# Fourth tile for transposed values, pauses in the modulation products, a longer lead for split weights and later norm products

## Chip, cores and metric

One Trainium2 chip, one of its cores. The metric is the device time of one execution in microseconds (us). Six engines matter: TensorE (PE in the profile, with its weight loads shown apart as PEld), VectorE (DVE), ScalarE (ACT), GpSimd (POOL) and SyncE (SP), whose queue issues every DMA of this kernel.

## What is computed

Two models in a row on 256 tokens of width 1024. The first block has two layers; each is a gated feed-forward (hidden width 2816), a hybrid mixer and a second feed-forward:

```
for l in range(DEPTH):                      # DEPTH = 2
    x = x + 0.5 * swiglu_ffn(rmsnorm(x, norm_ffn1[l]), ...)
    x = x + hybrid_mixer(rmsnorm(x, norm_mix[l]), ...)
    x = x + 0.5 * swiglu_ffn(rmsnorm(x, norm_ffn2[l]), ...)
```

The second block also has two layers. Both are modulated by products of a conditioning vector with a large matrix, `mod = silu(c) @ ada_w[i] + ada_b[i]`, once for the 256 tokens and once for 256 context tokens. Its first layer is a recurrence over time (`wkv_scan`, 16 heads of width 64, forward and backward), its second a differential attention. All of it is float32.

## The kernel before

**Layout and products.** Features lie on the partitions, tokens along the free dimension. A float32 product is made of three products in the float32r type: weights and operands are split into a high part and a low remainder (`whi`, `wlo` in the first block, `vhi`, `vlo` in the second), and high by high, high by low and low by high are added in PSUM (`mm3`, line 484). ACT makes the high part of a weight (`emit_hi`), DVE the low one (`emit_lo`, a subtraction of two SBUF tensors). A tile of the first block's weights is 128 by 1024, split in two pieces of 512 columns; it feeds 8 blocks of three products.

**The order of the instructions** is fixed when the program is built, by a planner. `Clock` holds an estimated time for each engine. `mm3` emits its three products and then calls `tick`, which lets every waiting chain whose estimated time has come emit its next step, and lets `Weights.tick` split more weights: a piece is emitted if its estimated time is below the PE clock plus `W.ahead` (2000 ns in the feed-forwards, 2000, 4000 and 2000 ns in the parts of a mixer), and if the ring has room (`RING`: 4 raw tiles, 5 split ones). A chain is a Python generator: work that hangs on one result, such as `swiglu` (line 697), the residual or a norm, and each `yield` ends a step. Tiles are taken with `grab` and returned with `give`; a chain that finds none waits. On the chip each engine runs its own list in order, so an instruction that waits holds up all that stand behind it.

**A feed-forward** (`ffn`, line 688) makes 44 products of 8 blocks each ("up": tiles a0, b0, a1, b1 ... b21), then 8 products of 22 blocks each ("down", n = 0 to 7). `done(j)` is called at the end of up-tile j and starts `swiglu(f)` after every second one; that chain needs the norm's factor `row.rstd`. Down product n = 0 needs all 22 results of `swiglu`, the last one in its last block. The passages spoken of below are the one from up to down and the one from a stage to the next, where the residual of n = 7 must be added before the next stage's norm and its last operand block are there.

**The norm.** `entered` (line 591) writes the split operand and adds squares on POOL into `sq`. After the eighth, `rstd_chain` (line 527) emits the PE product `ps<-mean,sq`, an addition on DVE, a power on POOL, a second PE product `ps<-ident,small` that spreads the factor over the partitions, and a copy into `rstd`; then `row.ready` is set.

**The modulation products** are chain `ada` (line 1094): 96 times a load of 256 KB, a POOL product of 128 by 1024 (`ada<-adaw,ada`) and two ACT sums. It is not urgent, starts 90 us in by the planner's clock, and takes a new product only while `self.calm` is true:

```
for n, (l, i, h) in enumerate(work):
    yield
    while not self.calm or there[n] > self.clock.t["PE"]:
        yield
```

`ffn` sets `calm` at its start and keeps it until down product 7; the mixers leave it false.

**The recurrence** (`rwkv`, line 1354) goes over eight pairs of heads j. Each has a chain `prepare`, two chains `products` (u = 0 for the context, u = 1 for the tokens), then `inverse` (small triangular inverses) and `recur` (eight steps, four for u = 0 and four for u = 1; each copies `rs` once). One set of tiles serves `inverse`, one `recur`. `products` ends with its own u's values: it transposes `q` four blocks at a time (`q<-ps` on ACT), grabs a tile `uv`, transposes `vp` (`ps<-ident,vp`) and copies the result into it:

```
uv, = yield from self.grab("uv")
```

`inverse` of a pair starts when both of its `products` have ended. `recur` gives a `uv` back after the four steps of its u. There are three such tiles (`NUV`).

Of the kernel before, what the change touches and what calls it, by code (L numbers as in the profile page):

```python
# [18 lines left out]
KD = 8  # L19
DFF = 2816  # L20
KF = DFF // 128
# [5 lines left out]
class Clock:  # L27
# [22 lines left out]
    def pressing(self):  # L50
# [6 lines left out]
        left = ((k + 1) * self.TICK - now) * (2.4 if fast else 1.2)  # L57
        short = self.FULL + PUSH - done
        if not 0 < short <= left:
# [79 lines left out]
class Part(tuple):  # L139


    t = 0.0
# [182 lines left out]
class Base:  # L325
# [66 lines left out]
    def between(self):  # L392

        if self.ranked and not (PUSH is not None and self.clock.pressing()):
            self.advance()

    def until(self, cond):
        n = 0
        t = self.clock.t
        while not cond():  # L400
            now = t["PE"]
            if self.tick():
                n = 0
            if t["PE"] == now:
                t["PE"] += 60
            n += 1
            assert n < 3000, (self.chains, {k: len(v) for k, v in self.free.items()})
# [76 lines left out]
    def mm3(self, ps, w, k, n0, xs, start, stop):  # L484
# [6 lines left out]
        if self.pace:  # L491
            self.paced = max(self.paced, self.clock.t["PE"] - SLACK) + self.pace
        wh, wl = hv[:, k, n0:n0 + 128], lv[:, k, n0:n0 + 128]
# [5 lines left out]
        mm(ps, wl, xs[0], start=False, stop=stop)  # L499
        self.tick(press=self.ranked and PUSH is not None and self.clock.pressing())  # L500

# [25 lines left out]
    def rstd_chain(self, row, ps=None):  # L527

        nc = self.nc
        m = row.n // 128  # L530
        summed = ps is not None
        if not summed:
            ps, = yield from self.grab("ps")
        s, = yield from self.grab("sm")
        if not summed:
            for t in range(m):
                nc.tensor.matmul(ps[:, 2 * t:2 * t + 2], row.sq[:, t * 128:(t + 1) * 128], self.mean,
                                 start=True, stop=True)
            yield
        nc.vector.tensor_scalar(out=s[:, 0:2 * m], in0=ps[:, :2 * m], scalar1=1e-6, scalar2=None, op0=ALU.add)  # L540
        yield
        nc.gpsimd.tensor_tensor(out=s[:, 8:8 + m], in0=s[:, 0:2 * m:2], in1=self.mhalf[:, :m], op=ALU.pow)
        yield
        for t in range(m):
            nc.tensor.matmul(ps[:, t * 128:(t + 1) * 128], s[:, 8 + t:9 + t].to_broadcast([128, 128]),
                             self.ident, start=True, stop=True)
        yield
        nc.vector.tensor_copy(row.rstd, ps[:, :row.n])
        self.give(s, kind="sm")
        self.give(ps, kind="ps")  # L550
        if row.half is not None:
            nc.scalar.activation(row.half, row.rstd, AF.Copy, scale=0.5)
        row.ready = True

    def square_sum(self, row, k, src):

        nc = self.nc
        if k == 0:
            row.ps, = yield from self.grab("ps")
            row.summed = 0  # L560
        s, = yield from self.grab()
        nc.scalar.activation(s[:, :row.n], src, AF.Square)
        yield
        while row.ps is None:
            yield
        row.summed += 1
        for t in range(row.n // 128):
            nc.tensor.matmul(row.ps[:, 2 * t:2 * t + 2], s[:, t * 128:(t + 1) * 128], self.mean,
                             start=row.summed == 1 and t == 0, stop=row.summed == KD, skip_group_check=True)
        self.give(s)  # L570
        if row.summed == KD:
            yield
            yield from self.rstd_chain(row, row.ps)
# [38 lines left out]


SLACK = 6000.0
PUSH = 0
MOST = 40
COST = 41, 47, 105, 77, 220, 200
# [7 lines left out]
class First(Base):  # L625
# [61 lines left out]

    def ffn(self, W, tag, l, after):
        nc = self.nc
        self.calm = True  # L690
        V, A = nc.vector, nc.scalar
        self.until(lambda: 0 in self.operand)
        xs = Lazy(self.operand, self.until, KD)
        hs = [[self.space(2 * i + j, F32R) for j in range(2)] for i in range(KF)]
        ready = {}

        def swiglu(pa, pb, f):
            while not self.row.ready:
                yield
            t, = yield from self.grab()  # L700
            h = t[:, :T]
            V.tensor_tensor(out=h, in0=pa[:, :T], in1=self.row.rstd, op=ALU.mult)
            self.give(pa, kind="ps")
            yield
            A.activation(h, h, AF.Silu)
            yield
            V.tensor_tensor(out=h, in0=h, in1=pb[:, :T], op=ALU.mult)
            self.give(pb, kind="ps")
            yield
            yield from self.hi_lo(*hs[f], h)  # L710
            ready[f] = self.part(*hs[f])
            self.give(t)

        held = {}

        def done(j, ps):
            held[j] = ps
            if j % 2:
                self.chain(swiglu(held.pop(j - 1), held.pop(j), j // 2))

        keys = [(tag, l, ab, i, 0) for i in range(KF) for ab in "ab"]
        self.product(W, keys, xs, done)
        if tag == "f2" and l == 1:
            self.enter_ctx()
        hl = Lazy(ready, self.until, KF)
        for n in range(KD):
            self.calm = n < KD - 1
            ps = self.take("ps")
            for k0 in (0, 8, 16):
                w = W.get((tag, l, "d", n, k0 // 8))  # L730
                for k in range(k0, min(k0 + 8, KF)):
                    self.mm3(ps[:, :T], w, k - k0, 0, hl[k], k == 0, k == KF - 1)
            self.chain(self.residual(n, ps, self.row.half, after))
# [53 lines left out]
    def mixer(self, W, l, after):  # L787
        nc, big = self.nc, self.big
# [175 lines left out]
        for t in range(NH):  # L964
            if t % 4 == 0:
                wg = W.get(("wax", l, t))
                n = min(4, NH - t)
# [17 lines left out]
            w = W.get(("gate", l, t, 0))  # L985
            self.gemm([(w, 0)], xs, lambda _, ps: self.chain(gate(t, ps)))
        W.lo_pool, W.hi_pool = MIXLO[3]
        W.ahead = 2000
        until(lambda: (3, 2) in pooled)
        for i in range(4):  # L990
            w = W.get(("pu", l, i))
            for j in range(2):
                n = 2 * i + j
# [38 lines left out]
HALF = [slice(64 * e, 64 * e + 64) for e in range(2)]  # L1032


NQ, NGE, NUV, NSH, NS, NPP = 8, 2, 3, 1, 9, 1
PACE, PACE_FROM = 0.0, 1
URGENT, RANKS = (1, 1, 1), (0, 0, 0, 0, 0)
NAQ = 12
# [1301 lines left out]
```

## Time and profile before

| what | us |
|---|---|
| median of 3 runs | 2267.69 |
| lowest and highest | 2259.29 and 2274.60 |
| profiled execution, its own time | 2270.05 |
| span of that execution in the trace | 2268.3 |

The span runs from the first to the last instruction. By the trace, the first block takes it up to about 1300 us (feed-forwards at 19 to 225, 435 to 658, 658 to 871 and 1080 to 1266 us, mixers between), the recurrence about 1300 to 2023 us, the attention the rest. A row of a stretch gives the busy time of each engine in it; "PEclk" is the share of its full clock that TensorE was granted, where 1.00 is 2.4 GHz and the lower of its two levels is 1.2 GHz. In a row of the timeline, the bracket at the end is the idle time of the engine before the instruction and what ended it.

### The profile page before, as it was taken

To read this page: it belongs to the slowest core of one execution; us is meant where nothing else is said; L and a number is where in the kernel's file an instruction comes from. 1 tells how busy PE (TensorE), PEld (TensorE's weight loads), DVE (VectorE), ACT (ScalarE), POOL (GpSimd) and SP (SyncE) were. 2 spreads that over 40 slices of the span, in tenths; PEclk is the share of its full clock that TensorE was granted. 3 is DMA by queue.
4 is the path that set the end of the run, shared out by engine and by line. 5 is a ranking of instruction groups with operands and counts; after the bars stand their busy time and mean duration, and the time that the engine had idled before them with its cause. 6 is when DMAs were issued, how large, how long until landed. Compare 5 with 4: busy or idle time off the path is not lost.

```text
span 2268.3 us, 46757 instructions
## 1 busy us (share of the span) xinstructions
PE 2076.7 (92%) x18172; PEld 1878.2 (83%) x18172; DVE 1704.9 (75%) x2903; ACT 1251.4 (55%) x2802; POOL 862.3 (38%) x1092
## 2 busy tenths in 40 slices
PE   7988998998889889989999988999899889889998
PEld 7988988998889789989999966777677667667787
DVE  6689898888888888898666666675775773657896
ACT  6666585666666666765556554343344342336665
POOL 1144555344454453562001144543552542312231
PEclk9999999999999999999999997897887887869999
DMA  7666454666666565545656310010110110215442
GB/s 244 205 188 201 157 167 127 211 217 196 199 212 210 190 199 191 157 151 188 199 187 179 121 61 29 25 43 30 34 33 29 32 40 29 62 41 159 138 130 85
DMA packets 114095, 300.38 MB, mean 132 GB/s; under 512 B 12624, under 2 KB 18512, under 8 KB 113744
## 3 DMA queue, kind: packets, MB, share of 16 engines
q1 hardware_dynamic: 113872, 297.39, 41.4%
q8 instruction: 142, 2.33, 0.4%
q14 instruction: 81, 0.66, 0.1%
HBM read 292.89 MB, written 4.46 MB: 131 GB/s over the span
## 4 chain that ended last, share of the span: by engine, by line
PE 53%; DVE 21%; ACT 9%; issue 8%; POOL 5%; DMA 3%; SPq 0%; ACTq 0%; DVEq 0%; POOLq 0%
PE ps L89 53%; DVE wlo L89 8%; ACT ada L89 3%; DVE t L89 3%; ACT whi L89 3%; DVE b L89 2%; DMA adaw<-in_ada_w_dram 2%; POOL ada L89 2%; DVE X L89 1%; DVE q L89 1%; DVE invN L89 1%; DVE ops L89 1%; DVE GE L89 1%; POOL invt L89 1%; POOL invX L89 1%
## 5 line engine op out<-in xcount | busy, mean ns | idle before, releaser
L89 PE MATMUL ps<-ops,whi 128*128 128x256 f32 x4852 | 893.1, 282 | 18.3 <-ACT ops L89 9.1
L89 DVE TENSOR_TENSOR wlo<-wraw,whi 128x512 fp32r<-128x512 f32 (+2 forms) x792 | 675.8, 891 | 147.5 <-ACT whi L89 142.5
L89 PEld LDWEIGHTS ps<-ops,whi 128*128 128x128 f32 x4852 | 756.6, 190 | 22.2 <-ACT ops L89 9.3
L89 PE MATMUL ps<-ops,wlo 128*128 128x256 f32 x2504 | 709.1, 283 | 29.1 <-DVE wlo L89 28.7
L89 ACT ACTIVATE whi<-wraw 128x512 fp32r<-128x512 f32 (+2 forms) x798 | 437.7, 597 | 127.3 <-issue 59.2
L89 PEld LDWEIGHTS ps<-ops,wlo 128*128 128x128 f32 x2504 | 475.5, 190 | 37.1 <-DVE wlo L89 36.8
L89 PE MATMUL ps<-b,whi 128*128 128x256 f32 x1580 | 322.3, 290 | 31.9 <-ACT b L89 17.1
L89 POOL TENSOR_TENSOR ada<-adaw,ada 128x1024 f32<-128x1024 f32 x96 | 237.7, 2476 | 266.0 <-ACT ada L89 184.7
L89 PEld LDWEIGHTS ps<-b,whi 128*128 128x128 f32 x1580 | 261.8, 197 | 36.5 <-ACT b L89 17.9
L89 PE MATMUL ps<-ops,vhi 128*128 128x512 f32 (+1 forms) x624 | 227.4, 441 | 0.0
L89 PE MATMUL ps<-b,wlo 128*128 128x256 f32 x712 | 206.1, 290 | 8.9 <-DVE wlo L89 5.4
L89 DVE TENSOR_TENSOR vlo<-vraw,vhi 128x512 fp32r<-128x512 f32 x202 | 144.8, 731 | 24.5 <-ACT vhi L89 21.3
L89 POOL TENSOR_TENSOR sq<-sq,t 128x256 f32<-128x256 f32 x49 | 45.2, 922 | 279.3 <-ACT t L89 278.8
L89 POOL TENSOR_TENSOR small<-small,mhalf 128x8 f32<-128x8 f32 (+3 forms) x62 | 72.3, 1169 | 204.6 <-DVE small L89 202.1
L89 PEld LDWEIGHTS ps<-b,wlo 128*128 128x128 f32 x712 | 139.7, 196 | 12.2 <-DVE wlo L89 8.2
L89 ACT ACTIVATE ada<-ada 128x512 f32<-128x512 f32 (+1 forms) x193 | 120.6, 626 | 51.9 <-POOL ada L89 51.3
L89 PEld LDWEIGHTS ps<-ops,vhi 128*128 128x128 f32 x624 | 120.6, 206 | 25.7 <-issue 0.7
L89 ACT ACTIVATE vhi<-vraw 128x512 fp32r<-128x512 f32 x202 | 121.5, 619 | 28.9 <-PE ps L89 16.6
L89 PE MATMUL ps<-ops,vlo 128*128 128x512 f32 (+1 forms) x312 | 135.0, 433 | 0.2 <-DVE vlo L89 0.2
L89 PE MATMUL ps<-vhi,ops 128*128 128x512 f32 x384 | 127.7, 413 | 1.8 <-DVE ops L89 1.1
L89 POOL TENSOR_TENSOR Sd<-S,small 64x128 f32<-64x128 f32 x61 | 27.5, 451 | 196.5 <-DVE S L89 194.5
L89 ACT ACTIVATE b<-t 128x256 fp32r<-128x256 f32 (+1 forms) x104 | 42.4, 413 | 101.8 <-DVE t L89 101.7
(314 smaller groups left out, 3433.1 us busy)
## 6 DMA issues: line engine op xcount, KB each, us to landing
wraw<-in_ffn_w_up_dram SPq DMA_DIRECT2D x175, 512.0 KB, 3.9
wraw<-in_w_in_dram SPq DMA_DIRECT2D x80, 512.0 KB, 3.7
wraw<-in_ffn_w_down_dram SPq DMA_DIRECT2D x64, 512.0 KB, 3.6
adaw<-in_ada_w_dram SPq DMA_DIRECT2D x96, 256.0 KB, 4.0
vraw<-in_da_in_dram SPq DMA_DIRECT2D x96, 256.0 KB, 2.7
vraw<-in_rw_in_dram SPq DMA_DIRECT2D x60, 256.0 KB, 2.6
wraw<-in_ffn_w_down_dram SPq DMA_DIRECT2D x32, 384.0 KB, 3.8
wraw<-in_w_lru_up_dram SPq DMA_DIRECT2D x32, 320.0 KB, 2.9
```

The lines of the kernel that those rows point to most:

```text
L89: return call(*args, **kw)
```

## The change

It has four parts, and a setting that makes room for one.

- `NUV` is 4: a fourth `uv` tile (2 KB per partition) in the recurrence. `dynamic_dma_scratch_size=1024` is passed when the program is set up; it shrinks an area in SBUF.
- `calm` is no longer set at the start of `ffn` but in `swiglu`, once the norm's factor is there; it is cleared after up-tile 38 (a19), five up-tiles ahead of the down products, and stays false in down product 0 as it did in 7.
- `W.ahead` becomes 5000 from up-tile 8 of each feed-forward, and in the last part of a mixer, in place of 2000.
- A norm whose squares were added on POOL puts off its first PE product by 2000 ns of the planner's PE clock, and its second by 1000 ns. `rstd_chain` is used so in the first block, for the context's norm and for the tokens' norm ahead of the attention.

```diff
         if not summed:
+            yield from self.later(LATER[0])
             for t in range(m):
...
         nc.gpsimd.tensor_tensor(out=s[:, 8:8 + m], in0=s[:, 0:2 * m:2], in1=self.mhalf[:, :m], op=ALU.pow)
         yield
+        if not summed:
+            yield from self.later(LATER[1])
         for t in range(m):
...
+    def later(self, ns):
+
+        t = self.clock.t["PE"] + ns
+        while self.clock.t["PE"] < t:
+            yield
...
+LULL, LEAD = 3, 5000
+LATER = 2000, 1000
...
     def ffn(self, W, tag, l, after):
         nc = self.nc
-        self.calm = True
...
             while not self.row.ready:
                 yield
+            if f < KF - LULL:
+                self.calm = True
             t, = yield from self.grab()
...
             held[j] = ps
+            if j == 8:
+                W.ahead = LEAD
+            if j == 2 * (KF - LULL):
+                self.calm = False
...
         for n in range(KD):
-            self.calm = n < KD - 1
+            self.calm = 0 < n < KD - 1
...
         W.lo_pool, W.hi_pool = MIXLO[3]
-        W.ahead = 2000
+        W.ahead = LEAD
...
-NQ, NGE, NUV, NSH, NS, NPP = 8, 2, 3, 1, 9, 1
+NQ, NGE, NUV, NSH, NS, NPP = 8, 2, 4, 1, 9, 1
...
-    nc = _bacc.Bacc("TRN2", target_bir_lowering=False, num_devices=1)
+    nc = _bacc.Bacc("TRN2", target_bir_lowering=False, num_devices=1, dynamic_dma_scratch_size=1024)
```

## Rows read from the trace of the kernel before

**Rows 1.** Stretches, the feed-forwards: busy PE, PEld, DVE, ACT, POOL; PEclk; DMA.

```profile
19.30:225.00 205.70, 192.98 (x1594) 190.40 (x1594) 162.20 (x280) 126.36 (x284) 64.01 (x106) 0.98 0.65 202
...
435.00:658.00 223.00, 198.35 (x1615) 194.03 (x1615) 192.36 (x235) 145.12 (x359) 106.34 (x49) 0.98 0.63 202
658.00:871.00 213.00, 192.50 (x1559) 188.98 (x1560) 181.22 (x231) 139.48 (x344) 94.98 (x44) 0.96 0.64 206
...
1080.00:1266.00 186.00, 186.00 (x1582) 185.85 (x1581) 123.01 (x237) 105.45 (x212) 13.04 (x15) 1.00 0.57 180
```

**Rows 2.** The same stretches, the modulation products' tiles alone (ACT, POOL).

```profile
19.30:225.00 205.70, 27.16 (x77) 47.34 (x19) 0.98 0.65 202
435.00:658.00 223.00, 53.13 (x160) 99.10 (x40) 0.98 0.63 202
658.00:871.00 213.00, 49.17 (x148) 88.35 (x36) 0.96 0.64 206
```

**Rows 3.** Waits of PE, 0 to 1301 us: total, times, longest.

```profile
PE ps L89 <- DVE wlo L89: 34.1, 40, 2.6
PE ps L89 <- ACT b L89: 17.1, 4, 6.2
PE ps L89 <- POOL sq L89: 12.1, 3, 6.7
```

**Rows 4.** Timeline of PE: up to down in the second feed-forward, then a norm.

```profile
587.53 0.58 PE L89 MATMUL ps<-b,whi 128*128 128x256 f32 x1 [6.22 <-ACT b L89]
589.99 0.58 PE L89 MATMUL ps<-b,whi 128*128 128x256 f32 x1 [1.88 <-DVE b L89]
...
659.88 1.02 PE L89 MATMUL ps<-mean,sq 128*128 128x2 f32 x4 [6.74 <-POOL sq L89]
```

**Rows 5.** Stretch of down products after that passage.

```profile
590.00:650.00 60.00, 60.00 (x480) 60.00 (x481) 54.81 (x67) 40.11 (x100) 31.18 (x16) 0.95 0.67 210
```

**Rows 6.** Timeline of DVE and POOL around one modulation product.

```profile
469.60 0.69 DVE L89 TENSOR_TENSOR wlo<-wraw,whi 128x512 fp32r<-128x512 f32 x1 [1.01 <-ACT whi L89]
...
471.35 2.53 DVE L89 TENSOR_TENSOR wlo<-wraw,whi 128x512 fp32r<-128x512 f32 x1 [0.72 <-ACT whi L89]
...
470.93 2.41 POOL L89 TENSOR_TENSOR ada<-adaw,ada 128x1024 f32<-128x1024 f32 x1 [3.81 <-ACT ada L89]
```

**Rows 7.** DVE groups, 495 to 570 us, then 1100 to 1175 us: busy, mean ns, idle.

```profile
L89 DVE TENSOR_TENSOR wlo<-wraw,whi 128x512 fp32r<-128x512 f32 x44 | 48.7, 1139 | 8.8 <-ACT whi L89 8.5
...
L89 DVE TENSOR_TENSOR wlo<-wraw,whi 128x512 fp32r<-128x512 f32 x54 | 34.9, 688 | 18.7 <-ACT whi L89 18.7
```

**Rows 8.** Timeline of ACT and DVE, pair 1; last, the copy of `q` of pair 2.

```profile
1411.60 0.58 ACT L89 ACTIVATE q<-ps 128x512 f32<-128x512 f32 x1
...
1430.38 0.91 ACT L89 ACTIVATE uv<-ps 64x512 f32<-64x512 f32 x2 [0.61 <-PE ps L89]
...
1431.53 1.93 DVE L89 STREAM_TRANSPOSE invN<-GE 32x1024 f32<-32x1024 f32 x1
...
1490.05 0.64 ACT L89 ACTIVATE q<-ps 128x512 f32<-128x512 f32 x1
```

**Rows 9.** Timeline of ACT, `recur`: first steps of pairs 0, 1, 7; a long step.

```profile
1405.61 0.36 ACT L89 ACTIVATE rs<-ps 64x256 f32<-64x256 f32 x1
...
1477.54 0.38 ACT L89 ACTIVATE rs<-ps 64x256 f32<-64x256 f32 x1 [1.12 <-PE ps L89]
...
1978.29 0.38 ACT L89 ACTIVATE rs<-ps 64x256 f32<-64x256 f32 x1 [2.89 <-PE ps L89]
...
1591.44 0.38 ACT L89 ACTIVATE rs<-ps 64x256 f32<-64x256 f32 x1 [1.88 <-PE ps L89]
1602.57 0.38 ACT L89 ACTIVATE rs<-ps 64x256 f32<-64x256 f32 x1 [5.77 <-PE ps L89]
```

**Rows 10.** Stretches of the recurrence: seven periods, and one piece without `recur`.

```profile
1405.00:1978.00 573.00, 527.57 (x6035) 413.73 (x6034) 361.81 (x672) 222.81 (x492) 245.68 (x445) 0.84 0.11 36
...
1864.00:1897.00 33.00, 27.25 (x461) 22.54 (x456) 16.95 (x27) 8.07 (x17) 12.86 (x20) 0.53 0.01 1
```

## Prediction

> **What bounds the kernel now.** I read it by stages, since the page's shares average over two quite different halves.
>
> The stretches of the four feed-forwards come first [rows 1]. They make the same products: some 1584 large ones each. The last takes 186 us, with PE busy in all of it and a clock of 1.00; the others take 205.7, 223 and 213 us, 83.7 us more than three times 186. What sets them apart is in [rows 2]: the modulation products run in these three (19, 40 and 36 of the 96; one falls in a mixer), none in the last. So the last shows what PE alone needs, and the 83.7 us are what the modulation products cost as they now lie. The stages are bound by PE, disturbed by DVE.
>
> How they disturb is seen in one product [rows 6]: a `wlo` subtraction on DVE takes 0.69 us alone, and 2.53 us when a POOL product of 2.41 us lies over it. Per product DVE is busy (192.36 - 123.01)/40 = 1.7 us longer [rows 1, 2]. In a stretch full of them `wlo` has a mean of 1139 ns against 688 ns, and DVE sits idle for only 8.8 us of 75, waiting for ACT's `whi` [rows 7]. PE's waits in the first block then follow [rows 3]: 34.1 us for `wlo`, 17.1 us for ACT's `b` (the last results of `swiglu`, at the passage from up to down), 12.1 us for the norm's squares on POOL. One passage is in [rows 4]: 6.22 and 1.88 us, 8.1 in all; the third feed-forward has the same two waits, the first one the remaining 4.7 us of ACT's `b` and 1.2 us more. The last, without modulation products, has none.
>
> The recurrence is another matter. `recur` of pair 0 begins at 1405.6 us and that of pair 7 at 1978.3 [rows 9]: seven periods of 81.8 us. PE looks full, 527.6 us of 573, but at a mean clock of 0.84, and with 0.53 where no `recur` runs [rows 10]. The chain that sets the period shows in [rows 8]: the last transposed block of pair 1 is copied at 1411.6 us, yet the copy into `uv` comes only at 1430.4, when pair 0 has ended its first four steps and given a tile back, and `inverse` begins at 1431.5. From the last copy of `q` to the copy into `uv` are 18.8 us here, and 13.9 to 24.9 in the seven pairs, 129 us in all. `inverse` then takes some 45 us until `recur` of pair 1 at 1477.5.
>
> **The change part by part.** The sum is against the profiled execution, 2270.05 us, which is 1.75 us longer than its span and 2.4 us above the median.
>
> *Pauses.* From a19 to down product 0 lie five up-tiles and one down product, 14 + 7.7 us at the pace of the last feed-forward (186/1584 = 0.117 us a product). At the pace of the second (40 in 223 us) this keeps out 4 products in each of three passages, and some 2 more at the start of the second and third until the norm is ready: 16 in all. The six that now overlap the passage hold DVE for about 10 us, more than the stall of 8.1. I take all of the 5.9 + 8.1 + 8.1 = 22 us. After such a stall PE is slower: 60 us for 480 products is 125 ns each, at a clock of 0.95 [rows 5], against 117; that is 4 us, I take 3 for all passages. **-25 us**, between -10 (half of the stall is older delay of DVE) and -30.
>
> *The 16 products that are put off* land in the last feed-forward, with their 16 loads on SP among those of the weights (DMA share 0.57 there, 0.63 to 0.65 where both run: room). Outside passages and norms one costs PE about (223 - 186 - 8.1 - 4.9)/40 = 0.6 us (4.9 us of the norm's wait lie in that stretch). DVE has 63 us idle there, they take 16 x 1.7 = 27; the first ones eat only the lead of the split weights. **+6 us**, between 0 and 16 x 1.84 = 29, when every lengthening (2.53 - 0.69) reaches PE.
>
> The Trainium skill has a rule against this move: by "SBUF — State Buffer", section "SBUF: two separate sides", DVE and GpSimd share a port pair as an exclusive lock, held for a whole instruction, against DVE operations with two SBUF inputs. By that rule a product costs the same wherever it is put. The 2.53 us beside 2.41 agree with it; the sum would take the +29.
>
> *The longer lead.* In the last feed-forward 2000 ns suffice for no wait at all, so it only matters beside modulation products. There it can put `whi` ahead of `swiglu`'s ACT steps and so fill DVE's 8.8 idle us of 75. PE waits 34.1 us for `wlo` in the first block, about 26 in these stages. DVE has still 48.7 us of `wlo` for 22 tiles, so most stays. **-8 us**, between 0 and -26. Nothing here excludes a loss: weights emitted earlier stand ahead of `swiglu` on DVE, and a late `swiglu` holds PSUM; at most the 3 us by which the lead grows, in each of three passages, +9.
>
> *Norms.* Of the waits of 6.74 us [rows 4] and 5.4 us (two others) up to 2 us each can be filled with products: **-4 us**. `rstd` comes some 3 us later, and with it every evacuation of the stage. In the feed-forwards PSUM's eight banks hold that; in the mixers DVE is the busier, and one starts its chain later: **+2 us**, from 0 to 6. The norm ahead of the attention lies beside other products (PE is busy in all of 2066 to 2120 us): nothing; without that cover, 3 us. The context's norm has 1000 us to spare: nothing.
>
> *Fourth `uv`.* `inverse` of the next pair no longer waits for half a `recur`; it starts when its `products` are done, 129 us earlier over seven pairs if all else stood still. What is late next: these `products` themselves, which need the `q` and `GE` tiles of the pair before last; they end about 89 us after its `recur` began (pair 2: the last copy of `q` at 1490.0 [rows 8] less 1405.6 [rows 9], and 4 us for the `vp` step), then `inverse` takes some 50: two periods in 139 us, 69.5 each, or 7 x 12.3 = 86 us less; with the first step 98. Against this stands PE: in 573 us it is idle for 45. I take 30 of the idle time and 10 for products at the full clock, where a stretch at 0.53 is now filled with other work. **-40 us**, between -98 and 0. The smaller scratch area changes nothing seen: every issue of a DMA in the trace is SP's.
>
> Sum: -25 + 6 - 8 - 4 + 2 - 40 = -69. 2270 - 69 = 2201; 2.4 less for the median: about **2200 us**.
>
> **Rivals.** (1) *PE is not full in the recurrence*, and the loop closes at 69.5 us. For it: 128 tiny products of `inverse` at a time may count as busy while they wait on one another, and PEld is busy in only 413.7 of 573 us, 72% [rows 10]; against it, the 92% of PE. -98 in place of -40: 2142 us. Here too stands a rule: "Perfetto Trace Analysis", section "Identifying the Most-Contended Engine", of the Trainium skill calls the busy share of matmuls a poor measure of headroom and the share of weight loads the better; by it this rival is the right one.
>
> (2) *PE is full in the recurrence*: `inverse` moves forward, and the large products that filled the time move back. Nothing comes of the fourth tile; the first block's -29 remain: 2239 us. For it: only 45 us of visible idle time, in many waits below 4 us.
>
> (3) *Slower: `inverse` in front of `recur` on DVE.* Its 32-row transposes take 1.9 to 2.2 us [rows 8], eight per pair, and `recur` goes through DVE several times in each step. Where two of them came in between, a step took 11.1 us [rows 9] instead of 7.1 (the mean over the trace, with u = 1 at 7.5 and u = 0 at 6.9). Now `inverse` lies beside all eight steps. The gain is at most 129/7 = 18.4 us a pair: it is lost when the eight steps grow by 2.3 us each. With all eight at 11.1 a pair loses 32 - 18.4 = 13.6: 7 x 13.6 = +95; with the first block's -29, 2334 us. Against it: four of the eight steps lie beside `inverse` today, and the two kinds differ by 0.6 us.
>
> (4) *The pauses only move the damage*: the put-off products cost their 29 us, the passages keep half their stall, and the lead gives nothing: -10 + 29 - 4 + 2 = +17, with -40 from the recurrence 2245 us.
>
> **How the numbers follow.** Forecast (2170 to 2235) 0.57; rival 1 0.14; rival 2 0.12; rival 4 0.09; rival 3 0.08. About 1%, 23 us, is what a measurement of this kernel can tell from no change. Faster by over 1% means below 2245: the forecast, rival 1, nearly all of rival 2 and half of rival 4, 0.78 with some off for widths; within 1% 0.13; slower 0.09. The range goes from the middle of rival 1, 2140, to 2256, which leaves out the rest of rival 1's side and rival 3.
>
> **What would show it.** Passages: no wait of PE for ACT's `b` above 1 us after the last up-tile. Modulation products: about 16 in the last feed-forward, which grows from 186 to some 192 us; the second and third shrink to 205 or less. Waits for `sq`: 6.74 becomes below 5. Recurrence: copy into `uv` within 3 us of the last copy of `q`, `inverse` starting before the fourth step of the pair ahead; periods of 75 to 77 us; PE's clock above 0.84. The prediction is wrong if the periods stay near 82 with `uv` no longer waited for (rival 2), fall below 71 (rival 1), or if single steps of `recur` pass 10 us often (rival 3); or if the last feed-forward passes 200 us (rival 4).

## The result, and the profile after

The changed kernel takes 2230.38 us (median of four runs, 2224.35 to 2237.65) against 2271.14 for the kernel before beside it: a ratio of 0.9845, 95% interval 0.9811 to 0.9878. It is faster by 1.5%, inside the range of the prediction (2140 to 2256 us), but half of the 3% that was forecast. The profiled execution of after has 2226.31 us and a span of 2224.5.

The six stages of the first block, after (start:end, duration, then busy PE, PEld, DVE, ACT, POOL, PEclk, DMA share and GB/s): feed-forward, mixer, feed-forward, feed-forward, mixer, feed-forward. They answer to [rows 1].

```profile
20.30:215.00 194.70, 188.09 (x1582) 186.26 (x1581) 152.98 (x278) 121.36 (x268) 57.46 (x102) 1.00 0.65 207
215.00:417.60 202.60, 188.67 (x1541) 184.39 (x1541) 182.03 (x312) 136.05 (x295) 108.22 (x137) 0.98 0.54 172
417.60:639.30 221.70, 200.89 (x1622) 195.54 (x1622) 191.01 (x234) 138.38 (x342) 97.81 (x45) 0.98 0.62 197
639.30:853.10 213.80, 195.49 (x1595) 190.41 (x1594) 182.44 (x228) 137.51 (x339) 93.16 (x43) 0.99 0.65 206
853.10:1056.40 203.30, 188.63 (x1543) 184.36 (x1542) 181.56 (x312) 135.32 (x295) 108.57 (x137) 0.98 0.55 172
1056.40:1248.20 191.80, 188.33 (x1586) 187.32 (x1586) 142.17 (x243) 115.89 (x253) 38.51 (x25) 1.00 0.60 185
```

The waits of PE in the first block, in the columns of [rows 3], then two places of the timeline of PE that answer to [rows 4]: the passage of the second feed-forward, and a norm.

```profile
PE ps L89 <- DVE wlo L89: 53.3, 59, 2.4
...
PE ps L89 <- POOL sq L89: 3.5, 3, 1.8
PE ps L89 <- ACT b L89: 2.7, 2, 1.8
```

```profile
571.86 0.93 PE L89 MATMUL ps<-b,whi 128*128 128x256 f32 x2 [1.75 <-ACT b L89]
...
642.25 0.61 PE L89 MATMUL ps<-mean,sq 128*128 128x2 f32 x4 [0.95 <-POOL sq L89]
```

Read together: the stalls at passages (17.1 us) and at norms (12.1) are nearly gone. Yet the second and third feed-forward stand at 221.7 and 213.8 us, as before, and the wait for `wlo` has grown from 34.1 to 53.3 us. By the same marks the six stages took 205.7, 209.8, 222.8, 213.4, 208.4 and 186.8 us before: the first feed-forward gives 11 us and the mixers 7 and 5, and the last feed-forward takes 5 back. The two mixers before:

```profile
225.00:434.80 209.80, 194.34 (x1548) 189.99 (x1548) 184.23 (x312) 135.05 (x295) 107.37 (x138) 0.96 0.52 166
...
871.00:1079.40 208.40, 193.15 (x1577) 188.34 (x1576) 182.18 (x312) 135.32 (x295) 106.02 (x137) 0.98 0.52 166
```

The recurrence after: the seven periods (1385.6 to 1920.6) as a stretch, as in [rows 10], and then the hand-over to pair 1, on ACT and on DVE, as in [rows 8].

```profile
1385.60:1920.60 535.00, 505.35 (x6016) 397.31 (x6015) 373.48 (x678) 220.61 (x488) 255.76 (x434) 0.87 0.12 36
```

```profile
1391.60 0.58 ACT L89 ACTIVATE q<-ps 128x512 f32<-128x512 f32 x1
...
1393.29 0.59 ACT L89 ACTIVATE uv<-ps 64x512 f32<-64x512 f32 x1
```

```profile
1394.68 1.96 DVE L89 STREAM_TRANSPOSE invN<-GE 32x1024 f32<-32x1024 f32 x1
```

`uv` follows the last `q` by 1.7 us instead of 18.8, and `inverse` begins 1.4 us later. Seven periods take 535.0 us instead of 572.7: 76.4 each. But `recur` of pair 7, from its first copy of `rs` to its eighth, has grown from 44.0 to 48.8 us, as its first steps show (ACT, first operation of the steps 0 to 3 of pair 7):

```profile
1920.56 0.38 ACT L89 ACTIVATE rs<-ps 64x256 f32<-64x256 f32 x1
1929.29 0.38 ACT L89 ACTIVATE rs<-ps 64x256 f32<-64x256 f32 x1 [3.04 <-PE ps L89]
1937.91 0.38 ACT L89 ACTIVATE rs<-ps 64x256 f32<-64x256 f32 x1 [3.72 <-PE ps L89]
1944.42 0.38 ACT L89 ACTIVATE rs<-ps 64x256 f32<-64x256 f32 x1 [4.70 <-PE ps L89]
```

Before, these three steps took 5.3, 6.2 and 6.5 us; now 8.7, 8.6 and 6.5. The groups of PE in that `recur` say what came in, first before (1978.3 to 2022.3), then after (1920.6 to 1969.4):

```profile
L89 PE MATMUL ps<-ops,vhi 128*128 128x256 f32 (+1 forms) x20 | 5.9, 386 | 0.0
...
L89 PE MATMUL ps<-ops,vlo 128*128 128x256 f32 (+1 forms) x10 | 3.4, 344 | 0.0
```

```profile
L89 PE MATMUL ps<-ops,vhi 128*128 128x512 f32 (+1 forms) x32 | 11.4, 447 | 0.0
L89 PE MATMUL ps<-ops,vlo 128*128 128x512 f32 (+1 forms) x16 | 6.4, 398 | 0.0
```

Eighteen large products that PE did within the seven periods before (667 there before, 649 after) now fall between the steps of pair 7, 8.5 us of PE's time. They are not the whole of the 4.8 us. f3 below is the changed kernel once more, with the same order of matmuls; its first step of pair 7 took 5.8 us at a granted clock of 1.00, where that of after took 8.7 at 0.61, a mean of the two levels 0.50 and 1.00 (the step in after, then in f3):

```profile
1920.60:1929.30 8.70, 8.70 (x49) 6.30 (x50) 3.84 (x9) 1.44 (x6) 0.39 (x1) 0.61 0.17 52
```

```profile
1920.10:1925.90 5.80, 5.80 (x50) 4.34 (x50) 3.89 (x9) 1.47 (x5) 0.40 (x1) 1.00 0.26 80
```

Before, this step had 1.00 too. In the second step of after PE is busy for 5.6 of 8.6 us; its longest wait there, 2.9 us, is for DVE's `S`.

Where the 43.8 us between the two spans lie, each term from the start or end of its stage in the two traces: the first block ends 18.0 us earlier (1266.6 to 1248.6), the start of the recurrence gives 2, the seven periods 37.7; `recur` of pair 7 takes back 4.8, the stretch to the last norm 0.5, and the attention behind that norm 8.6 (202.1 to 210.7). The last was no part of the forecast.

### The profile page after: what moved, and what is told of

Same layout as the page of the kernel before. It is cut to its first block, busy times and chain, and to the rows that moved or that the text cites. A ratio compares the mean times of both kernels' runs of the same rounds, so it can differ in the third digit from the quotient of the medians.

```text
span 2224.5 us, 46722 instructions
## 1 busy us (share of the span) xinstructions
PE 2056.4 (92%) x18172; PEld 1860.7 (84%) x18172; DVE 1729.4 (78%) x2915; ACT 1249.1 (56%) x2801; POOL 882.8 (40%) x1081
## 4 chain that ended last, share of the span: by engine, by line
PE 37%; DVE 23%; ACT 10%; issue 9%; POOL 7%; DMA 2%; DVEq 0%; ACTq 0%; POOLq 0%; SPq 0%
PE ps L89 37%; DVE wlo L89 9%; DVE t L89 3%; ACT ada L89 3%; ACT whi L89 3%; DVE b L89 2%; POOL ada L89 2%; POOL invt L89 2%; POOL invX L89 2%; DVE invN L89 1%; DVE X L89 1%; DVE ops L89 1%; ACT b L89 1%; ACT t L89 1%; DVE q L89 1%
## 5 line engine op out<-in xcount | busy, mean ns | idle before, releaser
L89 PE MATMUL ps<-b,whi 128*128 128x256 f32 x1580 | 317.2, 287 | 11.6 <-DVE b L89 6.7
L89 PEld LDWEIGHTS ps<-b,whi 128*128 128x128 f32 x1580 | 257.8, 194 | 15.6 <-DVE b L89 9.3
L89 DVE TENSOR_TENSOR vlo<-vraw,vhi 128x512 fp32r<-128x512 f32 x202 | 150.0, 758 | 25.0 <-ACT vhi L89 23.9
L89 PEld LDWEIGHTS ps<-vhi,ops 128*128 128x128 f32 x384 | 72.1, 194 | 20.5 <-DVE ops L89 2.6
```

Source lines behind the costliest of these rows:

```text
L89: return call(*args, **kw)
```

## The experiments

Each ratio is to the kernel before on the same chip. "Block" is the end of the first block in that run's trace, "attention" the time from the last norm to the end.

**Each part alone.** e1 is the kernel before with the fourth tile only:

```
-NQ, NGE, NUV, NSH, NS, NPP = 8, 2, 3, 1, 9, 1
+NQ, NGE, NUV, NSH, NS, NPP = 8, 2, 4, 1, 9, 1
-    nc = _bacc.Bacc("TRN2", target_bir_lowering=False, num_devices=1)
+    nc = _bacc.Bacc(..., num_devices=1, dynamic_dma_scratch_size=1024)
```

> Before with the fourth tile alone (and the smaller scratch area that makes room for it). Both theories: the first block as before, its last residual at about 1266 us, and periods of recur of about 76 us in place of 81.8. Theory A: the 14 us that the changed kernel loses behind the seventh period (recur of pair 7, then the attention) come with the fourth tile, since the order of all that follows is planned anew: about 24 us less than before in all, 2246 us. Theory B: they come from the late norm ahead of the attention, which this kernel has not: 38 us less, 2232 us.

2230.18 us, 0.9846 (0.9798 to 0.9894). Block 1263.9, period 75.9, `recur` of pair 7 48.5, attention 201.6. The tile alone gives all that the whole change does. The rest ends the first block 12 to 15 us earlier (1251.7 and 1248.6) and loses 9 of it in the attention; the intervals don't tell the remainder from nothing.

e2 is the changed kernel with three tiles (`NUV` = 3):

> The changed kernel with three tiles, so the edits of the first block and the late norm alone. Theory A: the first block ends as in the changed kernel (last residual at 1248 us, 18 us early), the periods return to 82 us and the attention is as long as before: 18 us less than before, 2253 us. Theory B: the attention is longer by some 9 us: 9 us less than before, 2262 us.

2260.83 us, 0.9978 (0.9961 to 0.9996). Block 1250.9, period 81.8, `recur` of pair 7 44.0, attention 209.9. Period and last `recur` go back together, so the longer last `recur` belongs to the fourth tile: it takes 44.0 us in both kernels with three tiles and 45.5 to 48.9 in those with four, apart from three traces of 55 us (see e7). Against e6 below the tile is worth 36 us, which the intervals don't tell from 40. That large products move back is rival 2's mechanism; in the trace of after it took at most an eighth of the gain.

e3 takes the norms' delay out of the changed kernel:

```
-LATER = 2000, 1000
+LATER = 0, 0
```

> The changed kernel without the putting off of norm products. Theory C: the second and third feed-forward gained nothing because the norm's factor comes 3 to 4 us later, so that swiglu starts with a backlog on DVE and the lead of the split weights is gone some 40 us sooner; without it they shrink by 6 to 8 us each and the first block ends 12 us earlier than in the changed kernel, 2218 us. Theory D: they gained nothing because the modulation products set DVE's pace there and a stall at the passage only absorbs what DVE owes; then both keep their 214 to 222 us, and the waits for the squares come back: 2 to 5 us slower than the changed kernel, 2234 us.

2218.19 us, 0.9799 (0.9769 to 0.9828). Block 1250.7, as with the delay. Its six stages, 216.9 (from the start of the span), 204.5, 215.4, 217.3, 210.1 and 186.6 us, show that the delay shifts time about: against the changed kernel the mixers and the third feed-forward are longer by 2 to 7 us, the second and the last shorter by 6 and 5. (f1, the same kernel, has 220.0, 206.4, 215.0, 217.4, 210.3 and 186.6.) The attention is down to 201.3, so its 8.6 us come from the delay.

e4 takes back the longer lead (`LEAD = 2000`):

> The changed kernel with the lead at 2000 ns as before. Theory E: the longer lead puts weights ahead of swiglu on DVE and gives back what the pauses saved: with 2000 ns the second and third feed-forward shrink by some 6 us each, 2218 us. Theory D: beside the modulation products the lead is gone whatever is planned: the feed-forwards stay within 2 us, and if the mixers' 7 and 5 us came from the longer lead they are lost: 2230 to 2242 us.

2217.14 us, 0.9798 (0.9765 to 0.983), block 1251.1. e6, the changed kernel once more, has 1251.7:

> The changed kernel itself, beside the others on the same chip: 2225 to 2232 us, first block up to 1249 us, 211 us of attention. Every theory expects this; it is the base for the other runs here.

2224.78 us, 0.9827 (0.9799 to 0.9854). Beside the delay the lead gives nothing in the block.

e5 takes back the pauses, that is, the three edits of `calm`:

```
     def ffn(self, W, tag, l, after):
+        self.calm = True
...
-            if f < KF - LULL:
-                self.calm = True
...
-            if j == 2 * (KF - LULL):
-                self.calm = False
...
-            self.calm = 0 < n < KD - 1
+            self.calm = n < KD - 1
```

> The changed kernel without its pauses: modulation products are taken from the start of a feed-forward to its down product 7 again. Theory F: the pauses are what shortens the first block; without them the stalls of 6 to 8 us at the three passages come back and its last residual is at 1264 to 1268 us in place of 1249: some 16 us slower than the changed kernel. Theory G: the first block's gain is that of the late norms in the mixers, and the pauses only move waits inside a feed-forward: it ends at 1249 to 1256 us, at most 6 us slower.

2249.29 us, 0.9921 (0.9896 to 0.9945). Block 1268.0 against 1251.7 of e6: beside lead and delay the pauses are worth 16 us. Ten products move to the last feed-forward by them (19, 41 and 35 in the first three and one in a mixer become 15, 36 and 35). Where the norms are not put off as well (e3), that stage takes 186.6 us with these ten, as it did with none. And without the pauses, lead and delay together give nothing: the block of e5 ends no earlier than that of e1 (1263.9), which has none of the three.

e7 has the fourth tile and the pauses only (`LATER = 0, 0`, `LEAD = 2000`):

> The fourth tile and the pauses, without the late norms and with the lead at 2000 ns. If late norms and longer lead bring nothing in sum in the first block (theory D), it ends at 1248 to 1252 us, the attention takes 201 to 202 us and the whole 2214 to 2219 us. If the two lengthen each other's gain, the first block ends later than 1256 us and the whole takes 2222 us or more.

2223.73 us, 0.9789 (0.9741 to 0.9837), block 1258.4, attention 202.0. Against e1 the pauses by themselves thus gave 5 us, not 16. And against e3 the lead by itself would have given 8. Its profiled execution took 2235.33 us, with 55 us in `recur` of pair 7, as in e5 and e9. f4 below is the same kernel and runs the same matmuls in the same order; there that piece takes 48.8 us. The last two steps tell the two apart, first e7, then f4:

```profile
1966.70:1984.80 18.10, 17.68 (x112) 16.20 (x112) 7.74 (x19) 4.54 (x14) 0.80 (x2) 0.50 0.14 43
```

```profile
1968.90:1980.60 11.70, 11.65 (x112) 10.58 (x112) 6.83 (x18) 4.09 (x13) 0.80 (x2) 0.83 0.08 24
```

The same 112 matmuls ran at the lower level of 1.2 GHz throughout in e7, at a mean of 0.83 in f4. So in e7 this lengthening is the granted clock's and not the kernel's; why the clock differed stays open.

**Lead and delay, with and without each.** Four kernels on one chip, all with the fourth tile and the pauses: the lead alone (f1, as e3), the delay alone (f2, as e4), both (f3, the changed kernel), neither (f4, as e7).

> Fourth tile and pauses, the long lead, norms not put off. Theory A (lead and delay fill the same waits, each is worth 7 to 8 us in the first block where the other is absent, nothing beside it): the first block ends at about 1251, 7 us ahead of the kernel with neither. Theory B (the lead gives nothing anywhere): it ends within 2 us of the kernel with neither.

> Fourth tile and pauses, the short lead, norms put off. Theory A: first block ends at about 1251, 7 us ahead of the kernel with neither, and at 210 us the attention is 9 us longer, so the time is about that of the kernel with neither. Theory B: the same end of the block as with lead and delay together.

> The changed kernel again. Theory A: first block ends at about 1251, as with lead or delay alone; 9 us behind the kernel with the lead alone, all of it in the attention. Theory B: as long as with the delay alone.

> Fourth tile and pauses, neither lead nor delay. Theory A: first block ends at about 1258, median about 7 us above the kernel with the lead alone. Theory B: 1251, and the 1258 of the earlier run was the scatter of one execution.

| | neither | lead | delay | both |
|---|---|---|---|---|
| block, this set | 1259.9 | 1255.8 | 1248.7 | 1251.6 |
| block, earlier | 1258.4 | 1250.7 | 1251.1 | 1251.7 |
| attention, this set | 201.0 | 201.4 | 211.3 | 209.0 |
| ratio | 0.9806 | 0.9809 | 0.9833 | 0.9822 |

(Intervals of the ratios: 0.9781 to 0.9832, 0.9775 to 0.9842, 0.9811 to 0.9855, 0.9791 to 0.9852.) Theory A holds for the block in its main point: the lead gives 4 to 8 us there where the norms are not late and nothing where they are, the delay 7 to 11 where the lead is short, and both together 7 to 8. They fill the same gap. The four times are not told apart: what the delay gives in the block it takes back in the attention. That the lead's few us do not show in the medians is within their intervals. The lead's 4 us in this set are also at the edge of what single traces tell: one kernel's block ends at 1250.7 and at 1255.8 (e3, f1).

**Which norm may be late.** e9 puts off only the norms ahead of the mixers, e10 only the one ahead of the attention (both with `LEAD = 2000`):

```
-            yield from self.later(LATER[0])
+            if getattr(row, "late", False):
+                yield from self.later(LATER[0])
...
+                self.row.late = gname == "norm_mix"
```

(the second call alike; e10 sets `late` on the row in front of the attention instead)

> The changed kernel with the norm put off only ahead of the two mixers, and the lead at 2000 ns. If the mixers' gain is that of the late norm, they take 202 to 205 us each as in the changed kernel, the second and fourth feed-forwards keep the 215 and 187 us that they have without late norms, and the attention its 201 to 202 us: 2210 us. If the mixers' times only drift with what goes before, there is no sum to be had: first block to 1251 us and 2216 us, as without any late norm.

> The changed kernel with the norm put off only ahead of the attention, and the lead at 2000 ns. Theory B: putting off that one norm changes the order in which the heads are planned, and the attention takes 209 to 211 us after the norm. Rival: the attention's 8 to 9 us come from the state in which the first block leaves the planner; then it takes 201 to 202 us here.

e9: 2207.5 us, 0.974 (0.971 to 0.977); mixers 201.4 and 204.4 us against 206.9 and 212.2 of e7, block 1245.6 against 1258.4, attention 202.8. e10, one execution: 2236.61 us, attention 210.7, the mixers 207.2 and 210.5. So the delay pays 13 us where it stands ahead of the mixers alone, and costs 9 us ahead of the attention; ahead of the second and the last feed-forward those stages grew by 7 and 5 us, while the third shrank by 6 (f2 against f4: 215.3 to 222.0, 186.8 to 191.3, 220.6 to 214.3). The interval of e9 lies clear of that of f4, the same kernel without any late norm (0.9781 to 0.9832), though not of e7's. Two stretches of equal place, 80 to 100 us behind the last norm, show how (columns as above), after first, then e3:

```profile
2093.80:2113.80 20.00, 15.16 (x103) 12.88 (x103) 12.91 (x33) 11.03 (x33) 4.65 (x6) 0.76 0.00 1
```

```profile
2093.40:2113.40 20.00, 18.93 (x130) 15.55 (x129) 15.89 (x39) 15.61 (x46) 4.68 (x6) 1.00 0.13 47
```

PE does 103 matmuls where it did 130. From the last norm to the end, its two longest groups of waits, again after and then e3:

```profile
PE ps L89 <- DVE aq L89: 7.6, 4, 2.6
PE ps L89 <- ACT aq L89: 5.6, 6, 2.0
```

```profile
PE ps L89 <- DVE aq L89: 4.7, 5, 1.4
PE ps L89 <- DVE small L89: 2.3, 1, 2.3
```

In e10 and e7, which differ by the delay of this one norm, PE runs the same matmuls in the same order up to 21 us behind the norm, and another order from there. In e10 (and in after) 96 matmuls of the heads (`aq`, `kq`) then run in one row, 76 to 92 us behind the norm, without the large `vhi` products between them; in e7 no such row is longer than 36 in this stretch. Products that depend on one another stand alone, PE waits, and its granted clock is 0.76 in place of 1.00. So the delay set another order, with 9 us more. That this order is the cost is how I read the rows; an order forced by hand was not tried.

**What holds the second and third feed-forward.** The prediction let the pace stay and took stalls away. e8 shortens POOL's modulation product to 32 of its 1024 columns, at the same price to the planner; PE, ACT and POOL run the same operations in the same order. It leaves out most of the modulation sums.

```
-            G.tensor_tensor(out=prod, in0=raw, in1=cb[:, :, 512*h:512*h + 512], op=ALU.mult)
+            self.clock.spend("G", COST[4] + 2.1 * 1024)
+            self.tc.nc.gpsimd.tensor_tensor(out=prod[:, :, 0:16], in0=raw[:, :, 0:16],
+                                            in1=cb[:, :, 512*h:512*h + 16], op=ALU.mult)
```

> The changed kernel with each of the 96 POOL products cut to 2 times 16 of its 2 times 512 columns, with the same cost in the planner, so that every engine keeps its order; loads and ACT sums stay. The modulation vectors are then sums over 16 of 512 columns. Theory D: what binds the second and third feed-forward is DVE, held up for the length of a POOL product; they fall from 222 and 214 us to 188 to 192 each, the first block ends near 1200 us, the whole takes some 2178 us. Theory H: the order binds, with the sums in front of swiglu's steps on ACT; they fall by less than 10 us each, the whole stays above 2205 us.

One execution: 2152.85 us. Second and third feed-forward of e8:

```profile
410.20:596.80 186.60, 186.49 (x1586) 186.29 (x1585) 122.82 (x234) 139.84 (x342) 16.70 (x44) 1.00 0.75 237
596.80:784.00 187.20, 187.20 (x1594) 187.20 (x1593) 121.25 (x229) 137.54 (x338) 17.11 (x43) 1.00 0.74 235
```

Both are at PE's own time. The DMA share is higher than ever, 0.75, and ACT is as busy as in the changed kernel, so neither the modulation's loads nor its steps on ACT cost anything by themselves: all of it comes with the length of POOL's operation, 2.4 us. The block ends at 1177.2, 74.5 us before e6. A long operation on POOL acts in two ways here, which e8 takes away together: DVE's operations get longer (191.0 us busy in the second feed-forward of after, 122.8 here), and ACT, in its own order, waits for POOL's product (20.3 us there, 1.4 here). How much of the gain is ACT's part was not tried apart.

e11 follows from that: e3 with the product on DVE.

```
-            G.tensor_tensor(out=prod, in0=raw, in1=cb[:, :, 512*h:512*h + 512], op=ALU.mult)
+            V.tensor_tensor(out=prod, in0=raw, in1=cb[:, :, 512*h:512*h + 512], op=ALU.mult)
```

> The changed kernel without late norms, and the modulation products computed on DVE in place of POOL. A product holds DVE for its own time, some 1.2 us by the 0.69 us of a 512-column subtraction, in place of 1.7 us of lengthening, and the planner knows of it. Theory D (DVE's time binds): DVE needs about 123 + 36 x 1.2 = 166 us in a feed-forward of 187, so the second and third fall to 190 to 200 us and the first block ends 30 to 45 us earlier, 2175 to 2190 us. Rival: what costs is not DVE's sum but the long single operation in front of swiglu and the weights; then one of 1.2 us costs half of one of 2.4 us and the first block ends 10 to 15 us earlier, 2205 us.

2149.07 us (2142.2 to 2157.28), 0.9495 (0.9458 to 0.9532): better than both kernels, with all of the work done. The products (shortest, median, longest in ns) and the two feed-forwards:

```profile
L89 DVE TENSOR_TENSOR ada<-adaw,ada x96: 1209/1218/1769, 116.6 to 1079.8; 128x1024 f32<-128x1024 f32 x96
```

```profile
409.50:596.20 186.70, 186.51 (x1587) 186.30 (x1586) 157.16 (x263) 137.89 (x330) 7.88 (x9) 1.00 0.72 233
596.20:783.50 187.30, 187.30 (x1595) 187.30 (x1594) 157.03 (x267) 136.65 (x330) 7.70 (x8) 1.00 0.73 232
```

DVE has the products to do itself and is busy for 157 us in place of 191 and 182. A product on POOL cost it 1.7 us of longer operations; its own takes 1.2, and it is placed between the splits instead of on top of one.

**Do the `q` tiles bind next?** e12 has ten of them (`NQ` = 10).

> The changed kernel with ten q tiles in place of eight. Theory I: what is late next in the recurrence are the q tiles of the pair before last, so products of a pair end sooner after recur of the pair before last begins (95 us in the mean now) and the period falls from 76 to 73 us or less. Rival: PE and the GE tiles hold the loop; the period stays within 1 us of 76 us.

One execution: 2221.41 us; period 76.8 against 75.9 of e6. They don't; what does hold the period at 76 us stays open.

## Why the prediction was off

The sum said -69 and the two profiled executions give -43.8. By its own steps:

- **Fourth `uv`, -40.** Right in its mechanism: `uv` 1.7 us behind the last `q`, periods 76.4 within 75 to 77, a clock of 0.87. In the seven periods it gave 37.7. But the 40 was made up otherwise, so that it came out nearly right is in part luck: I took 30 us of idle time and 10 for the clock, and the rows of the seven periods show PE idle for 15.8 us less (45.4 to 29.6) and busy for 22.2 less, some 8 of them the 18 large products that left. These went into `recur` of pair 7, which I had not foreseen: +4.8 with the clock's part in it. The last copy of `q` of pair 2 begins at 1474.3, 88.7 us after the `recur` of pair 0 (84.4 before), and the copy into `uv` ends its `products` 90.7 us after, near the 89 that I worked out from this pair; but the mean over the six pairs is 96. Its `inverse` began at 1478.0, and with fuller engines the mean from there to `recur` grew over the seven pairs from 51.9 to 56.9 us.
- **First block, -25 + 6 - 8 - 4 + 2 = -29: the steps that failed.** The trace of after gives -18, the repeats (e2, e4, e6, f3) some -15. The stalls went as described: a passage waits 1.75 us in place of 8.1 (my mark was 1), the norms 3.5 us in place of 12.1. What failed is "I take all of the 22 us": the pauses with their put-off products gave 5 us by themselves (e1, e7), 16 beside lead and delay (e5, e6), where I had 19. I added each edit as if the others were absent. The pauses on the one side and lead and delay on the other need each other: without the pauses the two gave nothing (e5 against e1). Lead and delay draw on one gap: they gave 7 to 8 together, near my 10, but not 8 and 2 each: the lead nothing beside the delay, the delay 7 to 11 without the lead. In the mixers, where I had the delay cost 2 us, it gained 13 (e9 against e7).
- **Why a removed stall did not come out.** The group of `wlo` between 495 and 570 us of after, as in [rows 7], looks as before:

```profile
L89 DVE TENSOR_TENSOR wlo<-wraw,whi 128x512 fp32r<-128x512 f32 (+1 forms) x46 | 48.3, 1081 | 8.8 <-ACT whi L89 8.5
```

 The same 8.8 us idle, nearly the same mean. The second and third feed-forward are paced by DVE, and perhaps in part by ACT, under POOL's operation (e8, e11), and PE's removed stall returns as a wait for `wlo`: 17.2 and 15.6 us in these two stages where there were 11.0 and 10.1. So the listed mark of 205 us or less was missed (221.7 and 213.8).
- **Put-off products, +6.** Ten, not 16, and they cost nothing (186.6 us with them in e3, f1). The last feed-forward's 191.8, which seems to answer to my 192, comes from its late norm: a mark met for a wrong reason.
- **The norm ahead of the attention at nothing: this failed too.** PE was busy around the norm, as I read, but the price fell far behind it, where the new order stands: 8 to 10 us (e3, e10, f2 against f4). The cover that I named was of the wrong stretch.

Of the rivals, 2 is refuted as a whole by e1 and e2. Rival 1 fell too: in the seven periods of after weight loads are busy for 397 of 535 us, 74%, and the loop stays at 76, not 69.5. The Trainium skill's "Perfetto Trace Analysis", section "Identifying the Most-Contended Engine", would read that share as headroom. The busy share of matmuls is 92% before and 94% after; which of the two tells more here is open, since what holds the loop at 76 was not found. Rival 3 decides where the steps of `recur` grow by 2.3 us; their mean went from 7.03 to 7.66 us (56 steps between `rs` and `rs` of the same pair), with five above 10 us where there were three: real, but at a quarter of that price. Rival 4 was right in that the first block gave far less, but not by its mechanism: the put-off products cost nothing, and the passages lost their stall.

The conclusion that I weighed against the pauses, that a product costs the same wherever it is put, did not hold for the put-off ones: ten in the last feed-forward cost nothing (e3). DVE is busy for 139.1 us there in place of 123.8, so it is held up there too, by 1.5 us a product, but it has the time. Where DVE has none, e8 and e11 agree with what stands behind it, the Trainium skill's "SBUF — State Buffer", section "SBUF: two separate sides": a DVE operation with two SBUF inputs and a GpSimd operation that reads SBUF exclude one another for a whole operation. With POOL's operations cut short, DVE's busy time in the second feed-forward fell from 191.0 to 122.8 us (e8). The 83.7 us that I read as the price of all 96 products were right: the first three feed-forwards of e8 take 84 us less than before. What I didn't draw from them is that these stages stay at DVE's pace wherever a stall is taken out.

## What to carry to other kernels

Where two engines lengthen each other's operations, price the whole of it by a stage without it, and try the faster engine for the work: a stall taken out of a stage that another engine paces comes back as a wait for that engine. Edits that draw on one gap must not be added up, and some give nothing without another; measure each with and without the others. A delay that a planner sees can cost in the order of work long behind it, so one that helps at some places should be given to these alone.

## What the runs showed of the hardware

The same product of two SBUF operands, 128 x 1024 in fp32, took POOL 2.41 us [rows 6] and DVE 1.22 us (e11). Moving 96 of them onto the busier engine shortened the kernel by 3% against e3, and in the second feed-forward that engine's busy time from 182.8 us (e3) to 157.2. In the attention a granted clock of 0.76 came with PE busy in 15.16 of 20 us, and 1.00 with 18.93 of 20. In two executions of one kernel the same 112 matmuls in the same order took 18.1 us at 0.50 and 11.7 at 0.83 (e7, f4).
